# One order for the weight stream's work, and SwiGLU tiles taken up inside the gate-up groups

## The chip, the cores and the metric

The kernel runs on one core of a Trainium2 chip. The metric is the device time of one execution in microseconds. Before the change three runs gave 1458.51 (median), 1458.33 and 1460.67 us.

## The reference

One encoder layer over 256 rows of width 2048. An input projection feeds four mixers side by side, then come an output projection, a cross attention to 256 memory rows, and a SwiGLU block; each adds to the residual, and a norm ends it. The change touches the SwiGLU block and the last slabs ahead of it:

```python
def swiglu(h, w_gate_up, w_down):
    gate, up = jnp.split(h @ w_gate_up, 2, axis=-1)
    return (jax.nn.silu(gate) * up) @ w_down
...
x = x + swiglu(rms_norm(x, norm_g[l, 2]), w_gate_up[l], w_down[l])
return rms_norm(x, final_norm_g)
```

`w_gate_up` is 2048 x 11264 and `w_down` 5632 x 2048, all in float32.

## The kernel before, in words

**Products in three matmuls.** A float32 product is made of three matmuls over values that were cut into a high part and a rest (lines 459, 460, 461, in `part`): high x wh, high x wl, low x wh. ScalarE makes wh with a cast, VectorE makes wl as weight minus wh (lines 153 and 154, or 165 and 166).

**The weight stream.** All weights lie in one array W in the order in which they are used, in slabs of 128 x 2048. `Stream._load` brings a slab into a `raw` buffer (SP's queue, line 123 or 126). `Stream._half` makes the parts of half a slab, 128 x 1024. `take` hands parts to the matmuls and first calls `_fill`, which keeps as many halves made ahead as the ring has wh/wl buffers: three of the pool `wp`, and more that are lent for a while (`wy`, `wz`).

**Plain and paired slabs.** Where a slab number stands in PAIRED, the slab goes through `_sums` and is used for a 2 x 2 block product in seven instead of eight products. Its four phases are: 1024 columns as loaded (phase 0); 512 columns (phase 1), followed by VectorE additions that combine quarters (line 176); 1024 columns (phase 2); 1024 columns of those sums (phase 3). For the slabs in SUMMED, all paired slabs of gate-up, one combination is prepared ahead in a tile t named res0 to res3. Two slabs ahead SP loads a quarter into t (line 113), ScalarE copies it (line 118), and a transfer from POOL's queue adds 1024 weight columns onto both halves (line 120). Then two additions are left on VectorE, the first of which reads t, and phase 2 casts t itself.

**The groups.** The gate-up product runs in eleven column groups. The first, of eight plain slabs, is done by `gemm_rows`. The other ten, numbered 1 to 10 here, are done by `paired_rows`, eight slabs each, by the plan NSSNSSNN (N plain, S paired), the tenth by NSNSNSNN. When a group's gate sums are complete, `mixed` and `gated` combine them and apply SiLU (lines 1106 and 1116). `upped` multiplies by the up half, VectorE transposes (line 584), and POOL stores two results in DRAM (`hidden`, line 586). That happens at the start of the next group.

**Tiles for down.** The down product needs the SwiGLU result as 44 tiles, split in high and low. `fetch` loads each tile from `hidden` into one of eleven tmp buffers (line 591, POOL's queue), and a later step splits it into `f` (line 317 on ScalarE, 309 on VectorE). Tiles 0 to 21 are fetched by `early`, tiles 22 to 43 by a second `fetch` that is added after the groups. The first down slabs use tiles 12 to 27.

**What sets the order.** Side work stands in `Background` as generators. Its `poll`, called after each product, steps a generator only when the planner's account of VectorE's owed time (`owed`) is below 0.9 us; `drain` steps to the end whatever the account says. `early` is one of these generators, and its `drain` comes after the tenth group. Beneath that, a scheduler puts the emitted instructions in order on each engine, by its own estimate of when operands are ready; engines and queues then work in that order. `keep_place` is the means to forbid it: a dependency without a semaphore on the engine's instruction that was emitted before.

Of the kernel before, what the change touches and what calls it, by code (L numbers as in the profile page):

```python
# [28 lines left out]
FT = DFF // P  # L29
# [14 lines left out]
GATE_UP = 1920 // 16 + 8  # L44
# [5 lines left out]
PAIRED = {a + i for a, plan in [(GATE_UP + 8 * j, GROUPS[j % len(GROUPS)]) for j in range(10)] + [(DOWN, PASSES[0]), (DOWN + 22, PASSES[1])]  # L50
          for i, x in enumerate(plan) if x in "Ss"}
# [25 lines left out]
class Stream:  # L77


    def __init__(self, tc, pools, W, bg):  # L80
        self.tc, self.nc, self.W, self.bg = tc, tc.nc, W, bg
        self.rawp, self.wp = pools
        self.order = []
        self.n = self.made = 0
        self.after = []
        self.halves = []
        self.at = self.phase = 0
        self.raw = None
        self.ring = [[self.wp, -1] for _ in range(3)]
        self.raws = [[self.rawp, -1] for _ in range(3)]  # L90
        self.sums = []
        self.places = []
        self.two = []
        self.begun = []
# [34 lines left out]

    def _half(self):  # L130

        nc, n = self.nc, self.made
        if n % 16 == 0 and self.phase == 0:
            self._load(n)
        if n // 16 in PAIRED:
            return self._sums()
        self.made += 8
        o = (n % 16) * P
        r = self.raw[:, o:o + 1024]
        if n >= NBLK - HELD:  # L140
            parts = []
            for a in (0, 512):
                wh, wl = self.places.pop(0)
                nc.scalar.copy(wh, r[:, a:a + 512])
                nc.vector.tensor_tensor(out=wl, in0=r[:, a:a + 512], in1=wh.bitcast(F32), op=ALU.subtract)
                parts.append((wh, wl))
            self.bg.dve(1024)
            self.halves.append(parts)
            return
        wh, wl = self._buffers(n, 1024)  # L150
        edges = [0, 256, 512, 1024] if n == 0 else [0, 512, 1024] if n == 8 else [0, 1024]
        for a, b in zip(edges, edges[1:]):
            nc.scalar.copy(wh[:, a:b], r[:, a:b])  # L153
            nc.vector.tensor_tensor(out=wl[:, a:b], in0=r[:, a:b], in1=wh[:, a:b].bitcast(F32), op=ALU.subtract)  # L154
        self.bg.dve(1024)
        self.halves.append((wh, wl))
# [123 lines left out]
class Block:  # L280
# [805 lines left out]
    def gate_up(self, gp, f, z):  # L1086

        nc = self.nc
        box, g, stored = {}, {}, []

        def gate(ps):
            for r in range(2):
                g[r] = gp.tile([P, 512], F32, name=f"g{r}", tag=f"g{r}")
                nc.scalar.activation(g[r], ps[r], AF.Silu, scale=box["col"][:, r:r + 1])

        def up(j, ps, h=None):
            h = h or [gp.tile([P, 512], F32, name="h", tag="h", bufs=2) for _ in range(2)]
            for r in range(2):
                self.stt(h[r], ps[r], box["col"][:, r:r + 1], g[r], ALU.mult, ALU.mult)
                self.store_turned(self.ff, 4 * j, r, g[r], h[r])  # L1100
            stored.append(self.bg.now)

        def mixed(q1, q5, q6, q7):

            g[0], g[1], h[0], h[1] = (gp.tile([P, 512], F32, name=n, tag=n, bufs=b) for n, b in (("g0", 1), ("g1", 1), ("h", 2), ("h", 2)))
            nc.scalar.copy(g[0], q1)
            self.tt(h[0], g[0], q6, ALU.add)
            self.tt(g[1], h[0], q7, ALU.add)
            self.tt(h[0], q5, h[0], ALU.subtract)
            self.tt(h[1], q5, g[1], ALU.subtract)  # L1110

        def gated(*ps):

            for r in range(2):
                self.tt(g[r], g[r], ps[r], ALU.add)
                nc.scalar.activation(g[r], g[r], AF.Silu, scale=box["col"][:, r:r + 1])

        def upped(j, ps):

            for r in range(2):  # L1120
                self.tt(h[r], h[r], ps[r], ALU.add)
            up(j, h, h)

        h = {}

        def fetch(k0, k1, ahead, pause, wait=0):

            m = {}
            for k in range(k0, k1 + ahead):
                if k < k1:  # L1130
                    while len(stored) <= k // 4:
                        yield
                    m[k] = self.tmp()
                    self.load_turned(m[k], self.ff, k)
                if k >= k0 + ahead:
                    while k0 == 0 and k - ahead >= 20 and "free" not in box:
                        yield
                    while wait and self.bg.now < stored[(k - ahead) // 4] + wait:
                        yield
                    mark = self.mark()  # L1140
                    self.split(f[k - ahead], m.pop(k - ahead))
                    self.keep_place(mark)
                    self.have = k - ahead + 1
                    yield pause

        def norm():

            mark = self.mark()
            nc.scalar.activation(self.mg[:, 0:1], self.mg[:, 0:1], AF.Silu)
            self.keep_place(mark)  # L1150
            yield 2.0
            self.row_norm(1, box)
            yield

        arp = ExitStack()
        ar = arp.enter_context(self.tc.tile_pool(name="arp", bufs=4))
        arrival = lambda: ar.tile([P, R], F32, name="ar", tag="ar")
        last = self.bg.add(self.arrive(self.xf[1], 3, arrival, self.put3, FAR), go=True)
        col = self.bg.add(norm())

        def combined():
            for ks, z in sums:
                yield 3.0
                yield from self.combine(z, *(self.h3[k] for k in ks))

        sums = [((2 * i, 2 * i + 1), z[(i + 1) % 4]) for i in range(4)]
        comb = self.bg.add(combined())
        whole = [self.whole(c) for c in range(4)]

        def before(n):  # L1170
            if n == 1:
                self.st.lend(self.wz)
                self.st.sums = list(whole)
            if n in (1, 3):
                self.bg.drain(self.late if n == 1 else last)
            if n == 3:
                self.leave(3)

        ps = self.gemm_rows("w_gate_up", [0, DFF], self.h3,
                            parts=[(range(8), [0]), (range(8, 12), [0]), (range(12), [1]), (range(12, 16), [0]), (range(12, 16), [1])],  # L1180
                            before=before)
        self.bg.drain(col)
        arp.close()
        more = ExitStack()
        rx = more.enter_context(self.tc.tile_pool(name="rawx", bufs=1))
        self.st.raws.append([rx, -1])
        gate(ps[0])
        up(0, ps[1])
        early = self.bg.add(fetch(0, FT - 22, 3, 2.0, 15))
        self.bg.drain(comb)  # L1190
        for j in range(1, DFF // 512):
            plan = GROUPS[(j - 1) % len(GROUPS)]
            if j == 10:
                box["free"] = True
            upped(j, self.paired_rows("w_gate_up", [j * 512, DFF + j * 512], self.h3, sums[:8 - plan.count("N")], plan, mixed, gated,
                                      before=lambda i: (j, i) == (10, 5) and self.st.back(self.wz, rx), swap=j % 2 == 0)[0])
        more.close()
        for c, x in enumerate(whole):
            nc.sync.dma_start(x, self.rd[:, c * 1024:(c + 1) * 1024])
        self.bg.drain(early)  # L1200
        self.fetch = self.bg.add(fetch(FT - 22, FT, 6, SOON))

    def down(self, f, sp):
# [752 lines left out]
```

## Time and profile before

| | |
|---|---|
| median of three runs | 1458.51 us |
| the profiled execution | 1461.85 us |
| its span | 1460.1 us |
| granted TensorE clock, mean | 0.995 |
| HBM read, written | 321.07 MB, 22.54 MB |

The profiled execution's own time is 1.75 us more than its span, and 3.3 us above the median.

A row of a stage table has the stretch in us from the span's start and its length; then, for TensorE's matmuls (PE), its weight loads (PEld), VectorE (DVE), ScalarE (ACT) and GpSimd (POOL), busy time with the number of instructions; then the granted clock, the DMA engines' share, and GB/s. A row of waits has the waiting engine and line, who released it, total us, times, and the longest. A row of a timeline has the start, the duration, engine, line, operation, tiles, how many were merged, and in brackets the idle time before it with its releaser. A row of groups has the busy time and mean ns of one, and then the idle time before them.

### The profile page before, as it was taken

What the parts mean: (1) busy time and instruction counts of PE and PEld (TensorE: products, weight loads), DVE (VectorE), ACT (ScalarE), POOL (GpSimd) and SP (SyncE); (2) the same over time, 40 slices, a digit from 0 to 9 for tenths busy, and PEclk for the clock granted to TensorE, in tenths of its full rate; (3) what the DMA queues carried; (4) which work ended last, traced back from release to release, by engine and by line L of the source; (5) the groups of instructions that cost most, each with busy time, mean ns of one, the idle gap of its engine ahead of it and who ended that gap; (6) DMA issues with size and microseconds to landing.
All of it is one profiled execution on the core that took longest, in us unless ns stands there. A gap on an engine that the chain in (4) does not pass through costs nothing.

```text
span 1460.1 us, 18662 instructions
## 1 busy us (share of the span) xinstructions
PE 1430.9 (98%) x6562; PEld 1176.1 (81%) x6562; DVE 1173.0 (80%) x1782; ACT 848.3 (58%) x1242; POOL 242.4 (17%) x315
## 2 busy tenths in 40 slices
PE   9999999999999999999999999999999998999997
PEld 7888888888888888888878777788888786788886
DVE  6677868777887676676668887999989987989997
ACT  7556655447555455565556555666666665655655
POOL 0000100012302233530412211111111016100000
PEclk9999999999999999999999999999999999999999
DMA  9787555466657788864978898898889988655564
GB/s 356 288 285 246 201 206 173 145 202 211 221 185 243 246 248 260 261 211 145 306 243 266 254 264 263 251 280 262 260 270 256 292 254 211 204 220 191 194 227 144
DMA packets 72461, 344.84 MB, mean 236 GB/s; under 512 B 10893, under 2 KB 12590, under 8 KB 45744
## 3 DMA queue, kind: packets, MB, share of 16 engines
q1 hardware_dynamic: 52976, 285.31, 55.6%
q0 software_dynamic: 18960, 57.69, 17.7%
q8 instruction: 51, 0.84, 0.2%
q10 hardware_dynamic: 432, 0.66, 0.1%
q14 instruction: 42, 0.34, 0.1%
HBM read 321.07 MB, written 22.54 MB: 235 GB/s over the span
## 4 chain that ended last, share of the span: by engine, by line
PE 72%; issue 11%; DMA 7%; DVE 6%; ACT 2%; POOL 2%; SPq 0%; POOLq 0%; ACTq 0%; DVEq 0%
PE pg L460 17%; PE pg L459 17%; PE pg L461 16%; PE pg L407 4%; PE pm L460 4%; PE pm L461 4%; PE pm L459 4%; DMA raw<-in_W 3%; DMA res<-in_W 2%; PE pg L408 2%; DVE wl L154 2%; DVE wl L166 1%; PE pm L1409 1%; DMA hidden<-g 1%; ACT wh L153 1%
## 5 line engine op out<-in xcount | busy, mean ns | idle before, releaser
L154 DVE TENSOR_TENSOR wl<-raw,wh 128x1024 fp32r<-128x1024 f32 (+1 forms) x395 | 474.3, 1213 | 163.8 <-ACT wh L153 161.6
L153 ACT CAST wh<-raw 128x1024 fp32r<-128x1024 f32 (+1 forms) x395 | 406.4, 1041 | 258.1 <-PE pg L461 183.8
L459 PE MATMUL pg<-wh,act 128*128 128x512 f32 (+1 forms) x1165 | 455.9, 392 | 1.7 <-ACT wh L153 1.6
L460 PE MATMUL pg<-wl,act 128*128 128x512 f32 (+1 forms) x1165 | 454.4, 390 | 2.3 <-DVE wl L154 2.3
L461 PE MATMUL pg<-wh,act 128*128 128x512 f32 (+1 forms) x1165 | 454.0, 390 | 0.9 <-DVE act L309 0.9
L459 PEld LDWEIGHTS pg<-wh,act 128*128 128x128 f32 x1165 | 219.2, 188 | 50.1 <-ACT wh L153 3.6
L460 PEld LDWEIGHTS pg<-wl,act 128*128 128x128 f32 x1165 | 219.0, 188 | 48.7 <-DVE wl L154 4.1
L461 PEld LDWEIGHTS pg<-wh,act 128*128 128x128 f32 x1165 | 218.8, 188 | 47.1 <-DVE act L309 1.5
L165 ACT CAST wh<-raw 128x1024 fp32r<-128x1024 f32 (+1 forms) x177 | 160.5, 918 | 162.5 <-DVE raw L176 66.1
L166 DVE TENSOR_TENSOR wl<-raw,wh 128x1024 fp32r<-128x1024 f32 (+1 forms) x177 | 182.7, 1059 | 37.5 <-ACT wh L165 37.1
L460 PE MATMUL pm<-wl,act 128*128 128x512 f32 x290 | 113.2, 390 | 0.2 <-DVE wl L154 0.2
L461 PE MATMUL pm<-wh,act 128*128 128x512 f32 x290 | 112.9, 390 | 0.0
L459 PE MATMUL pm<-wh,act 128*128 128x512 f32 x290 | 112.6, 390 | 0.0
L407 PE MATMUL pg<-act,wh 128*128 128x512 f32 x256 | 90.5, 396 | 0.0
L120 POOL DMA_DIRECT2D res<-in_W x39 | 34.8, 892 | 308.3 <-ACT res L118 239.5
L408 PE MATMUL pg<-act,wl 128*128 128x256 f32 x256 | 71.9, 281 | 0.0
L176 DVE TENSOR_TENSOR raw<-raw 128x512 f32<-128x512 f32 x99 | 68.2, 689 | 0.6
L460 PEld LDWEIGHTS pm<-wl,act 128*128 128x128 f32 x290 | 54.5, 188 | 12.1 <-DVE wl L154 0.7
L459 PEld LDWEIGHTS pm<-wh,act 128*128 128x128 f32 x290 | 54.4, 188 | 11.4 <-ACT wh L153 0.2
L461 PEld LDWEIGHTS pm<-wh,act 128*128 128x128 f32 x290 | 54.5, 188 | 11.2
L165 ACT CAST wh<-res 128x1024 fp32r<-128x1024 f32 x39 | 41.1, 1054 | 32.0 <-DMA res<-in_W 19.0
L407 PEld LDWEIGHTS pg<-act,wh 128*128 128x128 f32 x256 | 48.2, 188 | 10.4
(376 smaller groups left out, 1939.0 us busy)
## 6 DMA issues: line engine op xcount, KB each, us to landing
raw<-in_W SPq DMA_DIRECT2D x207, 1024.0 KB, 5.3
raw<-in_W SPq DMA_DIRECT2D x39, 768.0 KB, 6.3
res<-in_W POOLq DMA_DIRECT2D x39, 512.0 KB, 9.3
res<-in_W SPq DMA_DIRECT2D x39, 256.0 KB, 5.7
raw<-in_W SPq DMA_DIRECT2D x11, 512.0 KB, 7.1
hidden<-g POOLq DMA_DIRECT2D x22, 256.0 KB, 4.7
tmp<-hidden POOLq DMA_DIRECT2D x44, 128.0 KB, 7.3
features<-tmp POOLq DMA_DIRECT2D x32, 128.0 KB, 4.4
```

Of the source, the lines that this page charges most:

```text
L120: nc.gpsimd.dma_start(t, self.W[SUMS[1][n // 16]][:, 512:1536], accum_op=ALU.add)
L153: nc.scalar.copy(wh[:, a:b], r[:, a:b])
L154: nc.vector.tensor_tensor(out=wl[:, a:b], in0=r[:, a:b], in1=wh[:, a:b].bitcast(F32), op=ALU.subtract)
L165: nc.scalar.copy(wh, src)
L166: nc.vector.tensor_tensor(out=wl, in0=src, in1=wh.bitcast(F32), op=ALU.subtract)
L176: nc.vector.tensor_tensor(out=out, in0=a, in1=b, op=ALU.add)
L407: self.nc.tensor.matmul(p[:, :], wh, slot[:, :], start=start, stop=False)
L408: self.nc.tensor.matmul(p[:, 0:R], wl, slot[:, 0:R], start=False, stop=stop)
L459: self.nc.tensor.matmul(p, hi, wh, start=start, stop=False)
L460: self.nc.tensor.matmul(p, hi, wl, start=False, stop=False)
L461: self.nc.tensor.matmul(p, lo, wh, start=False, stop=stop)
L1409: self.b.nc.tensor.matmul(p, a, b, start=start and n == 0, stop=stop and n == 2)
```

## The change

It has two parts.

First, every instruction that `_half` emits, from twelve slabs ahead of the first paired group on, gets a dependency without a semaphore on the stream's previous instruction on the same engine. So the stream's casts on ScalarE, and its subtractions and additions on VectorE, keep the order in which they are emitted. Other work can still be placed between them.

Second, `early` is no longer in the background list. At the start of each of the first three plain slabs of a group one step of it is taken: at most one tile is loaded (four in the first step that loads) and at most one, three tiles behind, is split. What is left after the tenth group is stepped to the end as before. Its conditions stay: a load only after the group that makes its tile, a split only 15 us of planned TensorE time after that, the last two only from the tenth group on.

```diff
+        self.last = {}
...
     def _half(self):
...
-        if n // 16 in PAIRED:
-            return self._sums()
+        ins = self.nc.cur_bb.bb.instructions
+        mark = len(ins)
+        (self._sums if n // 16 in PAIRED else self._plain)()
+        if n // 16 < GATE_UP - 12:
+            return
+        for x in list(ins[mark:]):
+            if x.engine in self.last:
+                self.tc.add_manual_dep(x, self.last[x.engine], mybir.DependencyInfo(
+                    mybir.DependencyClass.NoSync, mybir.DependencyReason.DATA), reason="order")
+            self.last[x.engine] = x.name
+
+    def _plain(self):
...
-        early = self.bg.add(fetch(0, FT - 22, 3, 2.0, 15))
+        early = fetch(0, FT - 22, 3, 2.0, 15)
...
+            turns = [i for i, x in enumerate(plan) if x == "N"][:3]
+
+            def begin(i):
+
+                if (j, i) == (10, 5):
+                    self.st.back(self.wz, rx)
+                if i in turns:
+                    next(early, None)
+
...
-                                      before=lambda i: (j, i) == (10, 5) and self.st.back(self.wz, rx), swap=j % 2 == 0)[0])
+                                      before=begin, swap=j % 2 == 0)[0])
...
-        self.bg.drain(early)
+        for _ in early:
+            pass
```

`_plain` holds the rest of the old `_half`, unchanged. Note that `_load` runs ahead of the mark, so its transfers and the copy of line 118 are not themselves in the chain; the copy is still tied by `keep_place`. The instruction counts of all engines stay what they were.

More of the change, by code (lines that the diff above doesn't have):

```diff
@@ L130, in _half @@
     def _half(self):
-        nc, n = self.nc, self.made
+        n = self.made
         if n % 16 == 0 and self.phase == 0:
             self._load(n)
-        if n // 16 in PAIRED:
-            return self._sums()
+        ins = self.nc.cur_bb.bb.instructions
[9 more added lines that the diff above has]
+    def _plain(self):
+        nc, n = self.nc, self.made
         self.made += 8
```

## The prediction

> **What bounds it now.** I read the page first, then busy time by stage, then TensorE's waits stage by stage, then the order of time around one wait.
>
> ```profile
> span 1460.1 us, 18662 instructions
> PE 1430.9 (98%) x6562; PEld 1176.1 (81%) x6562; DVE 1173.0 (80%) x1782; ACT 848.3 (58%) x1242; POOL 242.4 (17%) x315
> ```
>
> TensorE works 98% of the span, and the change removes none of its instructions. All that can be won is time in which it waits or runs slowly. Those places lie in two stages, the ten paired groups of gate-up and the start of the down product; a stretch without any wait gives the pace.
>
> ```profile
> 781.10:1205.80 424.70, 416.63 (x1805) 337.78 (x1803) 376.20 (x438) 262.02 (x312) 60.93 (x71) 1.00 0.88 263
> 1205.80:1239.00 33.20, 26.52 (x101) 19.73 (x101) 25.27 (x49) 15.69 (x32) 20.82 (x24) 0.90 0.90 212
> 1239.00:1280.00 41.00, 38.84 (x162) 29.47 (x161) 38.65 (x72) 26.57 (x46) 7.03 (x8) 1.00 0.65 212
> 1285.00:1425.00 140.00, 140.00 (x619) 116.04 (x618) 128.92 (x184) 79.52 (x101) 0.00 (x0) 1.00 0.54 198
> ```
>
> The last row is the pace: 140.00 us for 619 matmuls, 0.2262 us each. The groups (first row) would need 1805 x 0.2262 = 408.2 us and took 424.7: 16.5 us lost. The start of down would need 22.8 and 36.6 us and took 33.20 and 41.00: 10.4 and 4.4 us lost. Together 31.3 us; that is the ceiling of any gain. VectorE is busy 376 of 425 us in the groups (89%): close behind, but not the bound.
>
> What ended the waits, first in the groups, then in 1205 to 1280:
>
> ```profile
> PE pm L460 <- DVE wl L166: 3.0, 4, 0.8
> PE pg L460 <- DVE wl L166: 2.3, 3, 0.8
> PE pm L459 <- ACT wh L165: 2.1, 4, 1.4
> ...
> PE pg L461 <- DVE f L309: 4.5, 2, 4.0
> PE pg L459 <- ACT f L317: 1.5, 1, 1.5
> PE pg L460 <- DVE wl L154: 1.3, 3, 0.5
> ```
>
> In the groups TensorE waits for the high and low parts (wh, wl) of paired slabs. In down it waits for f, tiles of the SwiGLU product that are taken up late.
>
> **The burst at the start of down.** Before, 20 of the 22 early tiles are split in one run there; the rows of 1205 to 1240 show 12 of them under the name f, others as z and act:
>
> ```profile
> L309 DVE TENSOR_TENSOR f<-tmp,f 128x256 fp32r<-128x256 f32 x12 | 4.6, 423 | 6.3 <-ACT f L317 6.2
> L317 ACT CAST f<-tmp 128x256 fp32r<-128x256 f32 x12 | 4.5, 403 | 11.3 <-DMA tmp<-hidden 11.2
> ```
>
> ScalarE waited 11.2 us there for loads: only eleven tmp buffers exist, so the later loads stand behind the splits of the earlier ones. The order of the changed kernel has all 22 splits inside the groups, the last one in group 10, and four loads in each of groups 1 to 7, three in group 8. So the first 10.4 us should go but for 0.3: the tiles that down begins with are ready, and the next ones (22 up) are loaded up to four groups ahead and are split between casts that wait for buffers TensorE frees. The other 4.4 us are mixed. Part waits for the low half of a plain slab whose second half the old order made first (the three waits for wl L154 above); the tie puts that right. Part is tiles 28 to 43 being late, which stays possible. Bounds 0 and 4.4 left; I take 2.0, near the middle, since neither cause has a row of its own for its sum. Saved: 10.1 + 2.4 = 12.5 us.
>
> What the splits cost in their new place: 22 x 0.40 us on ScalarE and 22 x 0.42 us on VectorE, three a group, 1.3 us on VectorE, which has some 4 us of each 41 free. They are no longer added to down, so the total is the same.
>
> **The loads in POOL's queue.** This is the price. POOL issues a group's product stores (hidden), the loads of tiles, and the accumulating transfers that complete the pre-added quarter of a paired slab (res). The second group of before already has the pattern that groups 1 to 8 now get:
>
> ```profile
> 829.85 1.56 POOL L586 DMA_DIRECT2D hidden<-g  x2 [4.03 <-DVE g L584]
> 831.41 0.96 POOL L120 DMA_DIRECT2D res<-in_W  x1
> 835.87 3.56 POOL L591 DMA_DIRECT2D tmp<-hidden  x4 [3.50 <-issue]
> 839.38 0.99 POOL L120 DMA_DIRECT2D res<-in_W  x1
> ```
>
> The first load waits in order until the store has landed. Behind it stand three loads and the transfer for the group's last paired slab, and behind that ScalarE's cast, VectorE's sum and two of the slab's four TensorE phases. That transfer goes out 9.5 us after the store. Its landing, and what TensorE lost:
>
> ```profile
> 851.58 1.05 ACT L165 CAST wh<-res 128x1024 fp32r<-128x1024 f32 x1 [3.38 <-DMA res<-in_W]
> ...
> 851.56 0.69 DVE L176 TENSOR_TENSOR raw<-res,raw 128x512 f32<-128x512 f32 x1 [1.83 <-issue]
> 852.66 1.23 DVE L166 TENSOR_TENSOR wl<-res,wh 128x1024 fp32r<-128x1024 f32 x1 [0.41 <-ACT wh L165]
> 853.80 0.69 DVE L176 TENSOR_TENSOR raw<-raw 128x512 f32<-128x512 f32 x1
> ...
> 852.37 0.39 PE L461 MATMUL pm<-wh,act 128*128 128x512 f32 x1
> 852.68 0.50 PE L459 MATMUL pg<-wh,z 128*128 128x512 f32 x1
> 853.94 0.51 PE L460 MATMUL pg<-wl,z 128*128 128x512 f32 x1 [0.76 <-DVE wl L166]
> 855.68 0.50 PE L459 MATMUL pg<-wh,z 128*128 128x512 f32 x1 [0.29 <-ACT wh L165]
> 856.94 0.50 PE L460 MATMUL pg<-wl,z 128*128 128x512 f32 x1 [0.76 <-DVE wl L166]
> ```
>
> It landed at 851.56. TensorE came to the quarter at 852.37 + 0.23 = 852.6 and waited twice: for this quarter's wl, and then for the next phase, whose second sum (853.80) the scheduler had put behind wl. [...]
>
> **The tied order** makes both sums first, then wl, then the next phase's cast. From the landing: two sums of 0.69 to 852.95, wl 1.2 more, about 854.1. TensorE's wl matmul comes some 0.2 later than the 853.94 of before, but the next phase has its wh at about 854.0 and its wl at 855.3, when TensorE reaches it. So the first wait stays (about 1.3 us) and the second (0.4 + 1.0) goes. The groups' own rows, cut at each group's first matmul (the second, third, seventh, ninth):
>
> ```profile
> 825.30:869.00 43.70, 41.89 (x182) 33.64 (x181) 37.66 (x45) 26.20 (x31) 8.56 (x11) 1.00 0.89 259
> 869.00:914.30 45.30, 43.16 (x182) 34.44 (x181) 37.92 (x46) 26.12 (x31) 7.91 (x10) 0.96 0.88 254
> 1039.50:1080.50 41.00, 40.90 (x181) 33.56 (x180) 36.62 (x44) 26.29 (x31) 4.73 (x7) 1.00 0.87 259
> 1121.40:1164.30 42.90, 41.84 (x182) 33.59 (x181) 39.42 (x47) 26.39 (x32) 5.93 (x7) 1.00 0.91 265
> ```
>
> At the pace they lost 2.5, 4.1, 0.1 and 1.7 us. Group 2 would lose 1.4 in the tied order. But a split (0.42) now stands on VectorE ahead of the transposes that release the store, so store, loads and landing come up to 0.4 later, and the store's own landing varies. I take 1.9 for each of groups 1 to 8, between 1.4 and 2.4, and 0.2 each for 9 and 10, which get no such loads and in which only the old order was to blame: 8 x 1.9 + 0.4 = 15.6, against 16.5 now. So 0.9 saved: the tie's gain is spent on the loads in five more groups. The bounds are wide: 0.3 a group if the store lands quickly (2.8 in all), 4.1 if each becomes like the third (33.2).
>
> The rest costs nothing: before 781 and after 1285 only neighbours change places, and in the last row of the stage table (no wait at all, with VectorE 92% busy) the four sums of a paired slab come behind its second wl instead of around it, so the third wl is no later. If that cover were gone, a plain wl (1.2 us) would show per slab. SP issues the same transfers, with one pair exchanged.
>
> **The sum.** 12.5 + 0.9 = 13.4 us. The profiled execution took 1461.85 us (its span 1460.1), 3.3 above the median 1458.51. 1461.85 - 13.4 - 3.3 = 1445.1.
>
> **Rivals.** That the change does not do what it says is excluded by its instruction order. A is this forecast. B: the loads cost the groups nothing, because stores land sooner or the earlier ScalarE copies release the transfers in time. For it: in group 7 the last transfer was also issued about 9 us after the store and 0.1 was lost. Against: there no tile loads moved ahead of it. Groups 2.8: 1458.5 - 13.7 - 12.5 = 1432.3. C, slower: TensorE's wait in every group grows past the point at which its clock is halved. These are stretches of 3.41 us, the last column but two the granted clock:
>
> ```profile
> 896.38:899.79 3.41, 1.26 (x5) 0.80 (x5) 2.52 (x3) 1.59 (x3) 0.00 (x0) 1.00 0.40 169
> 899.79:903.20 3.41, 3.41 (x9) 2.07 (x8) 2.39 (x3) 3.41 (x5) 0.00 (x0) 0.50 0.43 100
> 855.42:858.83 3.41, 2.39 (x9) 1.78 (x10) 3.17 (x3) 3.41 (x5) 0.48 (x1) 1.00 0.40 95
> 735.95:739.36 3.41, 2.12 (x8) 1.54 (x9) 3.41 (x5) 2.59 (x4) 0.00 (x0) 1.00 0.02 7
> ```
>
> After a stretch with 1.26 us of work the clock fell to 0.50 for the next one; after 2.39 or 2.12 it did not. The point lies between, near an idle time of 1.3 to 2.15 us. My 1.9 us is just below, and its pieces need not fall into one stretch. If all eight groups become like the third: 33.2 in the groups, 1458.5 + 16.7 - 12.5 = 1462.7. [...] D: tiles 22 to 43 take the burst's place, since they still are split in down: half of the 10.4 and all of the 4.4 stay, 1458.5 - 5.2 - 0.9 = 1452.4. Against it: their first loads now stand in groups 6 to 8.
>
> **Chances.** A 0.60 (1437 to 1452), B 0.14, D 0.12, C 0.09, and 0.05 for gains and losses that cancel. A difference of 0.2% (2.9 us) is about what a measurement of this kernel can tell. Faster 0.84, same 0.06, slower 0.10. The range reaches from the upper part of B to D: 1434 to 1456.
>
> **What would show it.** Right: no TensorE wait for f in the first 30 us of down; in 781 to 1206 one wait per group for wl L166 and none for the phase after it; VectorE two sums in a row, then wl. Wrong: the second stage row still 5 us over its pace (D); more than one stretch at clock 0.50 in the groups (C); groups 1 to 8 within 0.5 us of 40.9 (B); or waits for wl of plain slabs in the groups, which would mean that VectorE with its 1.3 us more became the bound.

## The result, and the profile after

The changed kernel took 1449.70 us (median of four runs, 1449.10 to 1453.54), the kernel before, beside it, 1459.59 us (four runs, 1458.33 to 1462.79). The ratio is 0.9935, with a 95% interval of 0.991 to 0.9959: 9.9 us faster, where 13.4 was forecast. The profiled execution of the changed kernel took 1453.54 us, 8.3 less than that of the kernel before. The lines of the casts, the subtractions and all behind them have moved by 13 (459 is now 472, 166 is 179, 176 is 189, 591 is 604), those of `_load` by one (118 is now 119, 120 is 121).

The page's head, then busy time by stage, with the same matmuls in the second and third row as in those of before:

```profile
span 1451.7 us, 18644 instructions
...
PE 1427.3 (98%) x6562; PEld 1178.6 (81%) x6562; DVE 1176.1 (81%) x1782; ACT 850.3 (59%) x1242; POOL 243.3 (17%) x315
```

```profile
779.10:1207.70 428.60, 417.78 (x1804) 341.89 (x1804) 384.06 (x455) 267.19 (x326) 78.47 (x90) 0.98 0.92 265
1207.70:1230.60 22.90, 22.90 (x101) 18.68 (x100) 18.41 (x29) 11.05 (x17) 4.17 (x5) 1.00 0.60 202
1230.60:1271.40 40.80, 38.65 (x162) 29.69 (x162) 38.29 (x71) 26.55 (x44) 7.02 (x8) 1.00 0.63 196
1285.00:1420.00 135.00, 135.00 (x596) 111.52 (x596) 124.41 (x171) 77.48 (x96) 0.00 (x0) 1.00 0.54 202
```

The pace is unchanged (135.00 / 596 = 0.2265). The first 101 matmuls of down run without a gap, 22.90 us for the 33.20 of before. The next 162 took 40.80 us, and 41.00 before: as good as nothing was won there. The groups took 428.60 us, 20.0 over their pace (1804 x 0.2265 = 408.6): more than before, not less.

What TensorE waited for, in the groups and then in 1205 to 1280:

```profile
PE pm L472 <- ACT wh L178: 5.9, 3, 2.7
PE pm L473 <- DVE wl L179: 2.8, 4, 1.0
PE pg L473 <- DVE wl L179: 2.0, 3, 1.0
...
PE pg L473 <- DVE wl L167: 1.1, 2, 0.5
PE pg L472 <- ACT wh L166: 0.5, 2, 0.3
PE pg L472 <- ACT wh L178: 0.3, 1, 0.3
PE pm L472 <- ACT y L338: 0.3, 1, 0.3
```

The waits for f are gone. In the groups the waits are fewer than before but longer, and three of them are for the cast itself (the longest 2.7 us). Here is that longest one, in group 7: GpSimd, ScalarE, VectorE and TensorE in order of time.

```profile
1041.85 1.57 POOL L599 DMA_DIRECT2D hidden<-g  x2 [6.03 <-DVE g L597]
1043.40 0.96 POOL L121 DMA_DIRECT2D res<-in_W  x1
1048.90 3.56 POOL L604 DMA_DIRECT2D tmp<-hidden  x4 [4.54 <-DMA hidden<-g]
1052.42 0.99 POOL L121 DMA_DIRECT2D res<-in_W  x1
...
1048.85 0.62 ACT L119 COPY res<-res 128x512 f32<-128x512 f32 x1
...
1065.65 1.04 ACT L178 CAST wh<-res 128x1024 fp32r<-128x1024 f32 x1 [6.33 <-DMA res<-in_W]
...
1065.63 0.69 DVE L189 TENSOR_TENSOR raw<-res,raw 128x512 f32<-128x512 f32 x1 [5.39 <-issue]
1066.36 0.69 DVE L189 TENSOR_TENSOR raw<-raw 128x512 f32<-128x512 f32 x1
1066.97 1.22 DVE L179 TENSOR_TENSOR wl<-res,wh 128x1024 fp32r<-128x1024 f32 x1
...
1066.75 0.80 PE L472 MATMUL pm<-wh,z 128*128 128x512 f32 x1 [2.70 <-ACT wh L178]
1068.24 0.80 PE L473 MATMUL pm<-wl,z 128*128 128x512 f32 x1 [0.70 <-DVE wl L179]
```

The stores go out at 1041.85. The tile loads wait for their landing until 1048.90 (the transfer of 1043.40 is for the paired slab before). ScalarE has made the copy by 1049.47, but the transfer that needs it stands behind four loads until 1052.42. It is used from 1065.63 on, 23.8 us after the store. VectorE then makes both sums ahead of wl, as the tie wants, and no second wait follows; but TensorE has stood since 1064.05, and its clock falls to 0.50. The last column but two of these stretches of 3.41 us is the granted clock:

```profile
977.79:981.20 3.41, 1.43 (x5) 0.99 (x6) 3.32 (x4) 2.95 (x4) 0.00 (x0) 1.00 0.51 216
981.20:984.62 3.42, 3.42 (x10) 2.64 (x9) 3.40 (x5) 3.42 (x5) 0.87 (x1) 0.50 0.83 264
...
1063.11:1066.53 3.42, 0.93 (x5) 0.43 (x3) 0.87 (x2) 0.88 (x1) 0.00 (x0) 1.00 1.02 372
1066.53:1069.94 3.41, 2.50 (x5) 1.70 (x6) 3.36 (x4) 2.94 (x5) 0.00 (x0) 0.50 0.30 103
1069.94:1073.35 3.41, 3.41 (x9) 2.64 (x9) 3.17 (x4) 3.06 (x5) 0.86 (x1) 0.50 1.09 285
```

In group 3 there is a third such place (at 892). Groups 3, 5 and 7 each had at least one stretch at half the clock: rival C in three groups of eight, and one of the prediction's own signs of being wrong.

### The profile page after: what moved, and what is told of

Read it like the earlier page. It is cut to its first block, busy times and chain, and to the rows that moved or that the text cites. A ratio compares the mean times of both kernels' runs of the same rounds, so it can differ in the third digit from the quotient of the medians.

```text
span 1451.7 us, 18644 instructions
## 1 busy us (share of the span) xinstructions
PE 1427.3 (98%) x6562; PEld 1178.6 (81%) x6562; DVE 1176.1 (81%) x1782; ACT 850.3 (59%) x1242; POOL 243.3 (17%) x315
## 4 chain that ended last, share of the span: by engine, by line
PE 75%; issue 13%; DMA 5%; DVE 3%; POOL 2%; ACT 1%; SPq 0%; POOLq 0%; ACTq 0%; DVEq 0%
PE pg L473 18%; PE pg L472 18%; PE pg L474 18%; PE pg L420 4%; PE pm L472 4%; PE pm L473 4%; PE pm L474 4%; PE pg L421 2%; DMA res<-in_W 2%; DMA hidden<-g 1%; DVE wl L179 1%; DMA raw<-in_W 1%; PE pm L1432 1%; POOL tmp L604 1%; POOL res L121 1%
## 5 line engine op out<-in xcount | busy, mean ns | idle before, releaser
L473 PEld LDWEIGHTS pm<-wl,act 128*128 128x128 f32 x290 | 54.4, 188 | 11.9 <-DVE wl L167 0.5
L420 PEld LDWEIGHTS pg<-act,wh 128*128 128x128 f32 x256 | 48.1, 188 | 10.5
```

What stands on the lines that cost most here:

```text
L420: self.nc.tensor.matmul(p[:, :], wh, slot[:, :], start=start, stop=False)
L473: self.nc.tensor.matmul(p, hi, wl, start=False, stop=False)
```

## The experiments

The theory after this: the tie wins in the groups, and the tile loads, which the early turns put ahead of the group's last accumulating transfer, take it away again. Its rivals: the splits on VectorE and ScalarE cost it; or the loads cost it wherever they stand. Each kernel was timed beside the kernel before on the same chip. The next table has, for the same matmuls in every kernel, the time from the first of a stage to the first of the next: A from the 2891st matmul row (at 600 us in the kernel before) to the first gate-up group's start at 745; B groups 1 to 9; C group 10 and the first 100 matmuls of down; D the next 161.

```
                        median    ratio to before (95%)       A       B       C       D
before                  1460.2    -                        145.1   383.0    74.7    41.1
before again (e12)      1460.1    one run                  149.0   377.7    74.5    42.2
changed                 1449.7    0.9935 (0.9910-0.9959)   142.7   386.9    64.4    40.8
changed again (e11)     1449.7    0.9925 (0.9900-0.9949)   142.7   381.8    64.4    40.8
e1  tie alone           1444.6    0.9888 (0.9870-0.9906)   142.6   368.4    74.9    40.8
e2  turns alone         1469.5    1.0061 (1.0036-1.0085)   147.6   399.8    64.3    40.1
e3  no early loads      1433.6    0.9831 (0.9807-0.9854)   142.7   368.8    64.4    40.7
e4  loads spread        1440.5    0.9857 (0.9837-0.9878)   142.6   375.9    64.4    40.8
e6  loads behind        1433.0    0.9809 (0.9791-0.9828)   142.6   367.0    65.3    40.7
e7  one per slab        1432.7    0.9809 (0.9790-0.9828)   142.7   367.0    66.1    40.7
e8  tie, ScalarE only   1455.4    0.9975 (0.9961-0.9988)   142.6   379.5    74.5    40.3
e9  tie, VectorE only   1451.5    0.9937 (0.9915-0.9959)   147.8   369.4    74.8    41.0
e10 loads, older store  1439.8    0.9849 (0.9826-0.9872)   142.7   374.2    64.5    40.8
```

The 1460.2 in the first row is the median of eleven runs beside e1 to e4; they lie between 1456.9 and 1464.8.

### e1: the tie alone

```diff
-        early = fetch(0, FT - 22, 3, 2.0, 15)
+        early = self.bg.add(fetch(0, FT - 22, 3, 2.0, 15))
...
-                if i in turns:
-                    next(early, None)
...
-        for _ in early:
-            pass
+        self.bg.drain(early)
```

> The tied order alone; the early tiles are again a background generator that is emptied after the tenth group, as before the change. If each part of the change does what its own step of the prediction says, the groups lose about 7 us instead of 16.5 (the second wait of a paired slab goes, and only groups 1 to 3 have tile loads), and the 12.5 us at the start of down stay lost apart from about 2: some 9 to 11 us below the time before the change, near 1449. If the gain of the changed kernel comes from the early turns alone, this one stands within 2 us of the kernel before.

1444.6 us: better than the changed kernel by 5.1. The tie alone wins 15.7 us, more than the step-by-step reckoning gave it, and the early turns on top of it lose. TensorE's waits in groups 1 to 9, and the two stages B and C (groups 1 to 3 of this kernel have 4, 4 and 3 tile loads):

```profile
PE pm L473 <- DVE wl L179: 0.4, 1, 0.4
PE pg L473 <- DVE wl L179: 0.3, 1, 0.3
```

```profile
778.10:1146.50 368.40, 367.64 (x1620) 303.96 (x1620) 343.19 (x394) 237.91 (x279) 55.97 (x65) 1.00 0.93 272
1146.50:1221.40 74.90, 68.00 (x284) 54.07 (x283) 60.33 (x89) 40.99 (x64) 26.02 (x30) 0.95 0.86 238
```

In 368.40 us TensorE stood still for 0.8. The burst at the start of down is all there: 74.9 us in C.

### e2: the early turns alone

```diff
-        (self._sums if n // 16 in PAIRED else self._plain)()
-        if n // 16 < GATE_UP - 12:
-            return
-        for x in list(ins[mark:]):
...
+        if n // 16 in PAIRED:
+            return self._sums()
```

> The early turns alone; the stream's instructions are ordered by the scheduler as before the change. By the prediction's steps the burst at the start of down goes (10 us less) and every group from 1 to 8 gets tile loads with both waits of a paired slab, 3 to 4 us each instead of 1.6 on average: 8 to 16 us more. So about the time before the change or up to 6 us above it, 1457 to 1464. If the tie is worth nothing, it stands at the changed kernel's 1449.7, within 2 us.

1469.5 us, 9.2 above the kernel before and 5.5 above the edge of what was expected. The burst is gone (64.20 us, without a gap), but the groups take 399.80. Stages B and C, then the waits in the groups:

```profile
782.80:1182.60 399.80, 381.56 (x1621) 304.20 (x1619) 347.78 (x416) 242.38 (x300) 73.68 (x85) 0.99 0.87 257
1182.60:1246.80 64.20, 64.20 (x284) 53.02 (x283) 52.96 (x70) 34.37 (x43) 8.48 (x10) 1.00 0.77 244
```

```profile
PE pm L460 <- DVE wl L166: 5.7, 8, 0.8
PE pm L459 <- ACT wh L165: 4.4, 6, 2.3
PE pg L459 <- ACT wh L165: 3.9, 6, 2.1
...
```

With e1 the four corners are there. The tie gains 15.7 us without the turns and 19.8 with them; the turns cost 9.2 without the tie and 5.1 with it. They win 10.4 or 10.5 in C and lose more in B: 16.8 or 22.1 untied (against 383.0 or 377.7), 13.4 or 18.5 tied (381.8 or 386.9 against 368.4).

### e3: no loads of the early tiles

```diff
-                    m[k] = self.tmp()
-                    self.load_turned(m[k], self.ff, k)
+                    m[k] = self.tmp() if k0 else self.h3[0][:, 0:R].bitcast(F32)
+                    if k0:
+                        self.load_turned(m[k], self.ff, k)
```

> The changed kernel without the loads of tiles 0 to 21: their splits stand where they were, but read a tile that is in the chip all the time, so the down product gets wrong values for these tiles. The groups of the changed kernel lost 20 us at the pace of 0.2265 us a matmul (428.6 - 1804 x 0.2265). If the tile loads cost them, what is left in groups 1 to 5 is under 0.5 us each and the time falls by 10 to 17 us, to 1433 to 1440. If the splits on VectorE and ScalarE cost them, the groups lose the same 20 us and the time stays within 3 us of 1449.7.

1433.6 us: groups 1 to 5 lose nothing, and B falls to 368.8, with every split where it was. So it is the loads, and not the splits, that cost the groups their 13 to 18 us. What is still lost, 0.3 us in group 7 and 1.6 in group 8, is lost in two groups in which the scheduler has put four loads of tiles from 22 on directly ahead of the last accumulating transfer; these loads e3 keeps. (Three of its five runs lie at 1433.4 to 1433.6 and two at 1439.9 and 1440.4; what the two had was not seen in a profile.)

### e4 and e7: the loads one by one, between the transfers

```diff
-                    while len(stored) <= k // 4:
+                    while len(stored) <= k // 4 + (k0 == 0):
                         yield
                     m[k] = self.tmp()
+                    mark = self.mark()
                     self.load_turned(m[k], self.ff, k)
+                    if k0 == 0:
+                        self.keep_place(mark)
```

> The changed kernel with each load of tiles 0 to 21 allowed one group later and held in its place in GpSimd's order, so that it no longer waits for the store issued just before it, and the loads stand one by one between the accumulating transfers instead of four in a row ahead of the last one. In the changed kernel that last transfer is issued 0.3 to 3 us after ScalarE's copy and takes 12.5 to 13.4 us from issue to first use in groups 2 to 8, against 9.7 to 10.8 us in groups 4 to 9 of the kernel before, which have no loads. If the loads' place in the queue or their overlap with this transfer costs the groups their 20 us, both go: issue to use falls to 10 or 11 us, and the time to 1435 to 1442. If the splits are the cost, no change (within 2 us of 1449.7). If loads cost wherever they stand, the loss only moves to the other paired slabs of the group.

1440.5 us. Groups 3 to 8 lose nothing, with three loads in each, so loads do not cost wherever they stand. What is left lies in two places. In group 2 (2.0 us) four loads come in one step, and the first split, held in its place, waits 2.84 us for one of them on ScalarE (at 830.45) ahead of the casts. In group 9 (7.0 us) it is the old mechanism with other loads; GpSimd at the end of group 8:

```profile
1094.86 0.87 POOL L121 DMA_DIRECT2D res<-in_W  x1 [15.52 <-ACT res L119]
1095.64 6.31 POOL L604 DMA_DIRECT2D tmp<-hidden  x7
...
1108.66 0.92 POOL L121 DMA_DIRECT2D res<-in_W  x1 [1.01 <-ACT wh L178]
```

The scheduler has put loads of tiles from 22 on ahead of an accumulating transfer that group 9 needs. It goes out at 1108.66, behind all of them; TensorE waited 3.4 us for its slab's wh. e7 takes both places away:

```diff
                     if k0 == 0:
                         self.keep_place(mark)
+                        if k < ahead:
+                            yield
+                    elif k < k0 + 8:
+                        self.tc.add_manual_dep(self.nc.cur_bb.bb.instructions[-1], box["late"], mybir.DependencyInfo(
+                            mybir.DependencyClass.NoSync, mybir.DependencyReason.DATA), reason="order")
```

(`box["late"]` is the name of GpSimd's last instruction at the sixth slab of group 10.)

> The spread loads again, with their two rough places smoothed: from the second group on one load at each plain slab and no four in a row, and the first eight loads of the second half held behind group 10's last accumulating transfer, so that they no longer stand in group 8 ahead of one. The spread kernel lost 2.0 us in group 2 and 7.0 in group 9 by its matmuls and nothing in groups 3 to 8. If the place of loads ahead of an accumulating transfer is what costs time, both go and the time is 1440.5 - 9 = about 1431 to 1434. If those 9 us are the price of the loads wherever they stand, they show up in other groups and the time stays at 1440.

1432.7 us, 11.9 us below the tie alone and 17 below the changed kernel. Stage B of e7:

```profile
778.00:1145.00 367.00, 367.00 (x1621) 303.89 (x1620) 347.65 (x412) 244.80 (x300) 66.22 (x76) 1.00 0.94 276
```

TensorE is busy for all 367.00 us: at 0.2264 a matmul this is the floor of the groups. The loads of tiles 0 to 21 and their splits are all in there, at no cost. Stage C, however, is 66.1 us and not 64.4: in group 10 ScalarE waits 5.59 us (at 1175.04) for a plain slab's own load. The first loads of the second half now stand there; that they are the cause is not shown.

### e6 and e10: behind the transfer, or ahead of it from an older store

```diff
-                if i in turns:
-                    next(early, None)
+                if turns[1:] and i == turns[1]:
+                    for _ in turns:
+                        next(early, None)
```

Beside this, e6 holds the loads in place as e7 does. e10 differs from e6 in two lines:

```diff
-                if turns[1:] and i == turns[1]:
+                if i == 2:
...
-                    while len(stored) <= k // 4:
+                    while len(stored) <= k // 4 + (k0 == 0):
```

> The changed kernel with its loads of tiles 0 to 21 moved behind the last accumulating transfer of the group (three steps at the second plain slab instead of one at each of three, held in place in GpSimd's order), and the first eight loads of the second half held behind group 10's last such transfer. The last transfer then goes out 0.3 us after ScalarE's copy, and the loads 1 to 4 us behind it, while it is on its way. If the longer way from issue to use in groups with loads (12.5 to 13.4 us against 10.8 or less) comes from standing behind the loads in the same queue, it is 10.8 or less here, the groups lose under 4 us in all, and the time is 1431 to 1436. If it comes from sharing the DMA engines, 12 us or more remain; use then comes at about 20.5 us from the store, at which the changed kernel's group 6 (20.9) lost nothing, so the time is 1432 to 1438 and ScalarE's cast shows a wait for the transfer of 1 to 2 us in most groups.

1433.0 us, and nothing lost in B. GpSimd in group 7, and ScalarE's use of the transfer:

```profile
1034.47 0.90 POOL L121 DMA_DIRECT2D res<-in_W  x1 [5.74 <-ACT res L119]
1035.22 2.88 POOL L604 DMA_DIRECT2D tmp<-hidden  x3
...
1045.26 1.05 ACT L178 CAST wh<-res 128x1024 fp32r<-128x1024 f32 x1
```

The transfer is issued as soon as the copy is made and is there when ScalarE comes to it, 10.8 us later; there is no idle time in the row. Three loads are under way at the same time. Seven of the eight groups with loads show 10.8 us, set by ScalarE's turn; group 3 shows 11.9, with a wait of 1.1 for the transfer. But group 3 waited for it in e3 too, where it has no loads (12.5 us). So loads that come behind it show no price in the groups. The trace's landings show the queue's transfers arriving in the order of their issue (all 305 of them in the profile of the kernel before and in the first of the changed one): here the accumulating transfer at 1045.0 and the three loads at 1046.6, 1048.4 and 1050.1; in group 7 of the changed kernel the four loads from 1055.5 to 1061.1 and the transfer behind them at 1065.5.

> The changed kernel's order of GpSimd's transfers within a group (store, store, one accumulating transfer, the tile loads, the last accumulating transfer), but the tiles loaded there come from the store of one group earlier, so that the loads wait for nothing and stand some 4 us earlier; their splits follow at once at the third slab. The first eight loads of the second half are held behind group 10's last accumulating transfer. If the wait for the store's landing is what makes the last transfer late, it goes out 0.3 us after ScalarE's copy, is used 10.8 us later or sooner, and the time is 1432 to 1435. If three or four loads in the queue ahead of it lengthen it whenever they are issued, 12 to 13 us from issue to use remain, ScalarE's cast waits 1 to 2 us for it in most groups, and as use comes at about 20.5 us from the store the time is 1433 to 1438.

1439.8 us, for one reason that neither theory had: in group 2 the first split waits 4.90 us on ScalarE for its tile, ahead of the copy, and 6.7 us are lost there, as in group 2 of e4. Groups 3 to 8 answer the question. GpSimd in group 6, and ScalarE:

```profile
996.34 3.08 POOL L604 DMA_DIRECT2D tmp<-hidden  x3
1002.70 0.92 POOL L121 DMA_DIRECT2D res<-in_W  x1 [3.29 <-ACT res L119]
...
1014.28 1.06 ACT L178 CAST wh<-res 128x1024 fp32r<-128x1024 f32 x1 [1.98 <-DMA res<-in_W]
```

The loads are issued by 999.4, 3.3 us ahead of the transfer, which waits for ScalarE's copy alone. Still it takes 11.6 us, and ScalarE waits for it. In the six groups it is 10.9 to 11.9 us with a wait of 1.1 to 2.1 each. With the loads behind it, the transfer was there after 10.8 at the latest but for group 3; directly behind the loads, in the two profiles of the changed kernel, it took 11.2 to 13.5 in groups 1 to 8, 12.5 in the mean. But groups 1 to 5 of e3 and 4 to 8 of e1 and e9 have no tile loads, and by its landing the same transfer took 9.6 to 11.6 us in them, 12.4 in group 3 of e3; here it landed after 10.8 to 11.8. So loads directly ahead of it lengthen it: in each of groups 1 to 5 the changed kernel's transfer took longer than e3's. That loads 3 us ahead do so is not shown, since the difference is within that spread. And the wait for the store brings the loads close and sends the transfer out up to 2.8 us late.

### e8 and e9: the tie on one engine

```diff
-        for x in list(ins[mark:]):
+        for x in [x for x in ins[mark:] if x.engine == mybir.EngineType.Activation]:
```

This is e8, on top of e1; e9 has `DVE`.

> The tied order alone, but for ScalarE's instructions of the stream only; VectorE's order is left to the scheduler. Tied on both engines the gain over the kernel before is 15.7 us. If what the tie wins comes from VectorE making both sums ahead of wl, as the prediction has it, most stays lost: 1454 to 1460. If it comes from ScalarE no longer casting a slab ahead of the one that is due (at 734 us of the kernel before it waits 6.0 us for a slab that is due later), this kernel has most of the gain, 1445 to 1449.

> The tied order alone, for VectorE's instructions of the stream only. Its subtractions follow ScalarE's casts, so this also binds what ScalarE may usefully do first. If VectorE's order is what counts, 1444 to 1447, as with both tied. If ScalarE's order counts for itself, 1450 or more. If either engine alone is enough, this one and the one with ScalarE tied both stand near 1445.

1455.4 us (ten runs, 1454.1 to 1461.5) and 1451.5 us (four, 1450.5 to 1452.0): each engine's order is worth something of its own, in another stage. With VectorE tied, B is 369.4, nearly that of e1, and A stays at 147.8. With ScalarE tied, A is 142.6 and B 379.5, within the two profiles of before. VectorE in group 2 of e8 does what it did before, with wl between the two sums:

```profile
847.74 0.69 DVE L189 TENSOR_TENSOR raw<-res,raw 128x512 f32<-128x512 f32 x1 [3.81 <-issue]
848.84 1.23 DVE L179 TENSOR_TENSOR wl<-res,wh 128x1024 fp32r<-128x1024 f32 x1 [0.40 <-ACT wh L178]
849.98 0.69 DVE L189 TENSOR_TENSOR raw<-raw 128x512 f32<-128x512 f32 x1
```

What ScalarE's order is worth in A shows in the kernel before, ahead of the groups:

```profile
734.25 2.94 ACT L153 CAST wh<-raw 128x1024 fp32r<-128x1024 f32 x3 [6.02 <-DMA raw<-in_W]
...
736.30 0.50 PE L459 MATMUL pg<-wh,act 128*128 128x512 f32 x1 [0.99 <-ACT wh L153]
737.75 0.50 PE L460 MATMUL pg<-wl,act 128*128 128x512 f32 x1 [0.95 <-DVE wl L154]
```

The first of the three casts is of a slab that was loaded later, and is used later, than the one whose two halves follow. The scheduler had put it first; ScalarE stood 6.02 us for its load, and TensorE for the slab behind it, whose own load had landed at 728.5. Tied, ScalarE casts the due slab at 731.88 (e1), and TensorE does not wait.

### e11 and e12: both kernels once more

> The changed kernel once more, unaltered, for a second profile. If the groups' losses (0, 1.7, 4.5, 1.2, 4.9, 0, 7.1 and 0.5 us in groups 1 to 8 of the first profile) come from when the last accumulating transfer lands, they should again follow its use: nothing up to about 21 us from the store, 1 to 2 us at 22.3, and 4 us or more from 22.8 on, with a stretch at half the clock. Which groups these are may differ, since the store's own landing varied between 4.8 and 7.1 us. Time 1448 to 1453.

1449.73 us (six runs). In groups 1 to 8, the time from the store to the first use of the last accumulating transfer, and the us lost against the same group of e7:

```
group             1     2     3     4     5     6     7     8
changed: use   21.1  22.3  22.8  22.2  23.0  20.9  23.8  21.5
         lost   0.0   1.7   4.5   1.2   4.9   0.0   7.1   0.5
again:   use   21.4  20.8  21.0  23.4  20.4  23.3  22.1  20.9
         lost   0.0   0.5   1.3   6.2   0.0   4.5   1.1   1.2
```

Use by 21.5 costs 0 to 1.3 us, at 22.1 to 22.3 it costs 1.1 to 1.7, and from 22.8 on 4.5 to 7.1. The groups have changed places. In the first profile the first tile load, which waits for the stores, went out 4.8 us after the first store in group 6, where nothing was lost, and 7.1 us after it in group 7, where 7.1 us were lost.

> The kernel before once more, unaltered, for a second profile. If the wait at 735 us comes from the order in which ScalarE casts the slabs there, it is there again, 1.4 us or more between 735 and 745; if it was chance, it is not. The groups again lose 14 to 20 us, by the same two waits for the parts of a paired slab.

The waits between 700 and 745 are there again, 3.1 us, and A is 149.0: no chance. Groups 1 to 9 lose 10.7 us over 367.0 here, 16.0 in the first profile; with group 10's first wait for f (1.5) 12.2, a little less than expected.

```profile
PE pg L459 <- ACT wh L153: 2.4, 1, 2.4
PE pg L460 <- DVE wl L154: 0.7, 1, 0.7
```

## Why the prediction was right in size, and where it was wrong

By the means of the two profiles of each kernel, stage by stage: A 147.1 to 142.7, B 380.3 to 384.3, C 74.6 to 64.4, D 41.6 to 40.8. That is -4.4, +4.0, -10.2 and -0.8, together -11.4 of the forecast -13.4; the whole executions differ by 11.0, the medians by 9.9 and 11.6.

**The burst: right.** 10.1 us were forecast and 10.2 came (in the window rows 33.20 to 22.90, with no wait for f left). Rival D fell: tiles 22 to 43 did not take the burst's place.

**The 2.4 us behind it: wrong.** "The tie puts that right" is the step that failed. The wait for the first plain half after a paired slab is still there, in all kernels (D is 40.1 to 42.2 everywhere). In the changed kernel:

```profile
1234.47 2.94 ACT L166 CAST wh<-raw 128x1024 fp32r<-128x1024 f32 x3 [1.52 <-PE pg L474]
...
1235.55 3.50 DVE L167 TENSOR_TENSOR wl<-raw,wh 128x1024 fp32r<-128x1024 f32 x3 [2.19 <-ACT wh L166]
...
1236.83 0.51 PE L473 MATMUL pg<-wl,act 128*128 128x512 f32 x1 [0.53 <-DVE wl L167]
```

ScalarE waited for TensorE to free a wh buffer and had then no time left: a matter of buffers, by this row, and not of order. That is argued, not shown: no run has changed the buffers.

**The rest "costs nothing": wrong, and the largest unforeseen gain.** "Before 781 only neighbours change places" overlooked that one of the neighbours waits 6.0 us for a transfer. The order of one cast was worth 2.4 us in the first profile and 6.3 in the second. The clock makes most of the difference: in the first TensorE waited 1.9 us there and the clock stayed at 1.00, in the second it waited 3.1 us and the clock was 0.50 for the next 6.83 us. In e2 and e9, where ScalarE's order is free too, A is 147.6 and 147.8, with 3.41 us at 0.50.

**The tie in the groups: right mechanism, too small.** The second wait went, as forecast, and VectorE's order did it (e9). That the first wait would stay at about 1.3 us was put on one group's numbers. It does stay when the transfer comes at 22 us or later; in e1, where the three groups with loads had it at 20.8 to 21.5, they lost 0 to 0.7 each.

**The loads: right mechanism, right mean, wrong spread.** Eight groups at 1.9 us make 15.2; measured 19.9 and 14.8. But hardly a group lost 1.9, so the mean fits by luck: the use varies by 3 us (20.9 to 23.8 us from the store in the first profile), and from 22.8 on the fall of the clock to 0.50 adds to the wait (of the 4.5 us of group 3 TensorE stood for 2.5, and its work took 2.0 longer).

Rival C was told as a whole or not at all, and came in three groups and in two. The stretch with 1.43 us of work was followed by half the clock, those with 2.12 and 2.39 before were not, so the point lies between. Two more stretches bring it closer: 1.66 us (e8, the stretch from 847.86) was followed by half the clock, 1.77 us (e4, from 831.00) was not. In idle time these two stretches had 1.75 and 1.64 us. The prediction called its 1.9 us a group "just below" the point; by its own rows, 1.3 to 2.15 us, it lay between them, and where it falls into one stretch it is more than the 1.75 us of e8.

Rival B, the groups with almost no price of the loads (2.8 us in all), gave 1432.3; it was held unlikely (0.14) by the loads' place alone, and e7, which has them in another place, measured 1432.7. That these two agree so closely is luck in part: e7 has the gain in A, which B lacks, and B has 12.5 us in down, where e7 won 9.4.

**What it amounts to.** The sum came out 2 to 3.5 us from the medians' difference because a gain that was not seen (4.4) made up for two that did not come, the 2.4 us behind the burst and the gain in the groups; that is luck. The verdict "the tie's gain is spent on the loads" was right, and the price understated: the tie alone is worth 15.7 us, and the turns as written take 5.1 of it back.

## What to carry to other kernels

Look, behind a queue worked in order, at what stands behind the newcomer, not at the newcomer: four loads that nobody was waiting for cost up to 7 us a group ahead of one transfer, and nothing in the groups behind it. When a scheduler by its own estimates orders work of fixed succession, look for the places where it puts a piece whose data is still under way ahead of one that is due, on every engine of the chain, since each engine's order was a loss of its own here. And when two edits come together, take each alone: here one was worth more than both.

## What the runs showed of the hardware

- TensorE's granted clock, in stretches of 3.41 us: it was 0.50 in the one after a stretch at full clock with 0.93, 1.24 and 1.43 us of TensorE's work (the changed kernel, from 1063.11, 889.04 and 977.79), 1.21 and 1.26 us (the kernel before, from 1206.99 and 896.38) and 1.66 us (e8, from 847.86). It stayed at 1.00 after 1.77 us (e4, from 831.00), 2.12 us (before, from 735.95) and 2.55 us (changed, from 933.41). A second slow stretch came where the first had 1.02 us of work (before, from 1210.40) and 2.50 us (changed, from 1066.53), and none where it had 3.12 us (changed, from 892.45) or 3.41 us (before, from 899.79).
- An accumulating transfer of 512 KB on GpSimd's queue landed 5.7 to 13.4 us after its issue in the changed kernel, 9.7 in the median of 39. For the last one of a group it was 11.1 to 13.4 us with three or four tile loads directly ahead of it (both profiles), 9.8 to 10.7 us in e6 with the loads behind it (11.8 in one group of eight), and 9.6 to 11.6 us without loads (groups 1 to 5 of e3, 4 to 8 of e1 and e9; 12.4 in one). The shortest one of the kernel before took 5.4 us.
- In groups 1 to 8 of the changed kernel's first profile the first tile load of a group, which waits for the group's two stores, went out 4.8 to 7.1 us after the first of them. The second store landed 3.4 to 5.7 us after its own issue.
